# A four-layer convolution and attention trunk: three instead of four convolution tiles on TensorE, more taps on GpSimd, other PSUM banks for the output accumulators

## The chip, the cores and the metric

The kernel runs on one core of one Trainium2 chip. The metric is the device time of one execution in microseconds; lower is better. The core's engines run their own instruction queues in order and wait for one another through semaphores: PE (TensorE, matrix products), DVE (VectorE), ACT (ScalarE), POOL (GpSimd), and SP, which here only issues DMAs.

## The reference, cut to what matters

The input is 512 positions of 1024 channels. Four residual layers follow one another, of kinds A, B, C, A. Each computes x + Mixer(RMSNorm(x)); the inner width is 2048, so 16 tiles of 128 channels. The change concerns kind A, in layers 0 and 3:

```python
def conformer_conv_mixer(h, w_in, conv_w, conv_b, ln_g, ln_b, w_out):
    proj = h @ w_in
    val, glu_gate, z = jnp.split(proj, 3, axis=-1)
    u = val * jax.nn.sigmoid(glu_gate)
    u = causal_depthwise_conv(u, conv_w) + conv_b      # 31 taps, each channel by itself
    u = jax.nn.silu(layer_norm(u, ln_g, ln_b))         # over the 2048 channels
    return (u * jax.nn.silu(z)) @ w_out
```

Kind B is forgetting attention with 16 heads, kind C a short convolution of three taps. Both also end with a product by their `w_out`. All arithmetic is float32 in accuracy: each matrix product is made of three passes (high part by high part, high by low, low by high).

## The kernel before, in words

**Layout.** Everything stands transposed: 128 channels on the partitions, 512 positions along a row. Weights arrive in chunks of 128x1024 (`w_raw`). ACT casts a chunk to its high part (`w_hi`), and POOL or DVE subtracts to get the low part (`w_lo`, line 413). In an A layer, up to the layer norm, only POOL does that. A chunk feeds 24 products of 128x128 by 128x512 on PE, 8 in each of the three passes. An A layer uses 48 chunks for `val`, `gate` and `z` of the 16 tiles, and 16 chunks for the output product. `z` of a tile is multiplied nine tiles after its `val` and `gate` (`LAG`), so a stock of `z` products is left when the convolution ends.

**The convolution of a tile i.** ACT writes tap 0 into a PSUM bank (`cv`). DVE adds one tap after another there (`scalar_tensor_tensor`, line 341). The first `POOL_TAPS[i]` taps are taken from it: for each of them ACT writes u times the tap's weight (`prod`) and POOL adds it to `pacc` (line 330). At the end DVE adds `cv`, the bias and `pacc` to give `d`. Tile 0 has no POOL taps. Tiles in `PE_TILES` go another way (`conv_pe`): ACT reorders u, DMAs write it to DRAM and read it back as four phases, PE applies 36 matrices of 128x128 loaded by nine DMAs (`pw`, in a ring of 8 slots), and DMAs and ACT undo the reordering.

**The layer norm.** POOL sums the tiles and their squares into `s1` and `s2` (`count_in`); the last three tiles (`DIRECT`) are not added there. PE sums over the channels, with two products (`meanp`, `e2p`) for `s1`, `s2` and two more for each of the last three tiles. Tiles 0 to 3 and those on PE first get a shift `m0` added on POOL. From the sums ACT and DVE make `lnrp`, one over the standard deviation. Then for each tile DVE subtracts the mean and multiplies by `lnrp`, ACT applies SiLU, POOL multiplies by `sz` (SiLU of `z`; DVE does it for the first two tiles), and ACT and DVE split the result into `g_hi` and `g_lo`.

**The output product** (`out_projection`). Its first half runs over pairs of tiles and keeps four accumulators `o0` to `o3` open in four PSUM banks; each pair is 24 products. The second half makes `o4` to `o7` one after another.

**PSUM.** There are eight banks in five groups: `mm` has 3, `acc` 2, `tr`, `sum` and `o` one each. Within a group, banks are handed out in turn, and who gets one waits until its former user has been read. `val`, `gate` and `z` use `mm`. The convolution's tiles use `acc`, `o`, `acc`, `tr` in turn. `sum` holds `e2p`, `o` holds `meanp`, and the last user of `acc` ahead of the output product is `lnrp`.

**The order of the work.** All steps are recorded and then put in order by a planner (`Plan`), which has costs for each step and engine, priorities (`boost`) and numbers of slots; the order of each engine's queue is fixed when the program is built. Any change of taps or tiles thus moves many instructions.

Of the kernel before, what the change touches and what calls it, by code (L numbers as in the profile page):

```python
# [19 lines left out]
ND = D // P  # L20
# [5 lines left out]
NEG = -1e30  # L26
LAYERS = ("A", "B", "C", "A")
LAG = 9
POOL_TAPS = (0, 5, 5, 5, 5, 5, 5, 5, 5, 5, 5, 5, 5, 5, 5, 5)
PE_TILES = {0: (6, 10, 13, 15), 3: (6, 10, 13, 15)}  # L30
NP = 4
NL = (KC - 1 + NP - 1) // NP + 1

# [217 lines left out]
def trunk(ctx: ExitStack, tc: tile.TileContext, x, w, vec, pw, out):  # L251
# [14 lines left out]
    def name_(s):  # L266
        count[0] += 1
        return f"{s}_{count[0]}"

    def slot(name, dt=F32, ring=(None, 1)):  # L270
        n = name_(name)
        return plan.buf(lambda: big.tile([P, T], dt, tag="big", name=n, bufs=N_SLOTS), *ring,
                        slot=True)

    def psum(tag, name):
        n, k = name_(name), PSUM_BUFS[tag]
        return plan.buf(lambda: ps.tile([P, T], F32, tag=tag, name=n, bufs=k), "ps_" + tag, k)
# [15 lines left out]
    def pe_time(n):  # L293
        return max(0.108, 0.0105 + n * 0.4225e-3)
# [80 lines left out]
    def mms(jobs, dst, cost, reads, boost=0):  # L375

        def fn(e):
            for o, a, b, start, stop in jobs():
                nc.tensor.matmul(o, a, b, start=start, stop=stop)  # L379
        plan.op({"pe": cost}, fn, reads, dst, boost)  # L380
# [141 lines left out]
                hh[d], hl[d] = split(f, f"hn{self.layer}_{d}", ("dve",), boost=-2000)  # L522
            return hh, hl

    def out_projection(layer, gh, gl, make_g, spare_bank):

        last_layer = layer == len(LAYERS) - 1
        nxt = None if last_layer else Stream(layer + 1)
        half, pairs = ND // 2, NE // 2

        def evac(d, acc):
            tt(("dve",), xs[d], acc, xs[d], A.add)
            if last_layer:
                plan.op({"dma": 0.9}, lambda e, d=d: nc.sync.dma_start(out[d], xs[d]()), [xs[d]])
            else:
                nxt.add(d)

        accs = [psum("mm" if d < 3 else spare_bank, f"o{d}") for d in range(half)]
        for j in range(pairs):
            hi, lo = chunk()  # L540
            for kk in range(2):
                make_g(2 * j + kk)
            for g, (a, b) in enumerate(((hi, gh), (hi, gl), (lo, gh))):
                for kk in range(2):
                    k = 2 * j + kk
                    mms(lambda a=a, b=b, g=g, kk=kk, k=k: [
                            (accs[d](), a()[:, kk * 512 + d * P : kk * 512 + (d + 1) * P], b[k](),
                             k == 0 and g == 0, k == NE - 1 and g == 2) for d in range(half)],
                        accs, pe_time(T) * half, [a, b[k]])
        for d in range(half):  # L550
            evac(d, accs[d])
        for d, tag in zip(range(half, ND), ("o", "acc", "acc", "mm")):
            acc = psum(tag, f"o{d}")
            for hf in range(2):
                hi, lo = chunk()
                for g, (a, b) in enumerate(((hi, gh), (hi, gl), (lo, gh))):
                    mms(lambda a=a, b=b, g=g, hf=hf, acc=acc: [
                            (acc(), a()[:, k * P : (k + 1) * P], b[8 * hf + k](),
                             hf == 0 and k == 0 and g == 0, hf == 1 and k == 7 and g == 2)
                            for k in range(8)],  # L560
                        [acc], pe_time(T) * 8, [a, *(b[8 * hf + k] for k in range(8))])
            evac(d, acc)
        return nxt


    def conformer(layer, st):
        lo_engines["now"] = ("pool",)
        on_pe = PE_TILES[layer]
        FIRST, EARLY = 2, 7
        raw_tiles, SPREAD, SHIFTED, DIRECT = 2, 12, 4, 3  # L570

        def cw(i, s):
            return v(f"conv_w{layer}", i * KC + KC - 1 - s)
# [22 lines left out]
        def conv(i):  # L596

            n_pool = POOL_TAPS[i]
            pacc = pool_part(i, n_pool) if n_pool else None
# [10 lines left out]
        def conv_pe(i):  # L610


            n, m, C = on_pe.index(i), T // NP, P // NP
            first = -2000 if i == NE - 1 else 0
            u, acc = us[i], psum(tags[i % 4], f"cv{layer}_{i}")
            d2[i] = slot(f"d{i}")
            ua, r, oa, ob = (slot(nm) for nm in ("ua", "phases", "oa", "ob"))
            ud, od = (plan.buf(lambda nm=nm: scratch.tile([P, T], F32, name=nm))
                      for nm in (f"ud{layer}_{i}", f"od{layer}_{i}"))

            def swap(src, dram, dst):

                plan.op({"dma": 2.5}, lambda e: nc.sync.dma_start(dram(), src()), [src], [dram], first)
                for k in range(NP):
                    plan.op({"dma": 0.5 if k < NP - 1 else 1.5}, lambda e, k=k: nc.sync.dma_start(
                        dst()[k * C : (k + 1) * C, :].rearrange("c (a m) -> c a m", a=NP),
                        dram()[:, k * m : (k + 1) * m].rearrange("(a c) m -> c a m", a=NP)),
                        [dram], [dst], first)

            plan.op({"act": 0.65}, lambda e: nc.scalar.copy(  # L630
                ua()[:, :].rearrange("p (h m) -> p h m", h=NP),
                u()[:, :].rearrange("p (m h) -> p h m", h=NP)), [u], [ua], first)
            swap(ua, ud, r)
            jobs = [(g, lag) for g in range(NP) for lag in range(NL)]
            for k in range(0, len(jobs), 4):
                mats = slot("pw", ring=("pw", 8))
                plan.op({"dma": 0.8}, lambda e, mats=mats, k=k: nc.sync.dma_start(
                    mats(), pw[n if layer == 0 else len(PE_TILES[0]) + n, k // 4]), w=[mats])
                mms(lambda mats=mats, k=k: [
                        (acc()[:, g * m + lag : (g + 1) * m], mats()[:, q * P : (q + 1) * P],  # L640
                         r()[:, g * m : (g + 1) * m - lag], lag == 0, lag == NL - 1)
                        for q, (g, lag) in enumerate(jobs[k : k + 4])],
                    [acc], 0.87, [mats, r], boost=first or SPREAD * (k // 4))
            act(oa, acc, None, boost=first)
            swap(oa, od, ob)
            vb, at = v(f"conv_b{layer}", i)
            plan.op({"act": 0.7}, lambda e: nc.scalar.activation(
                d2[i]()[:, :].rearrange("p (m h) -> p h m", h=NP),
                ob()[:, :].rearrange("p (h m) -> p h m", h=NP), AF.Identity,
                bias=vb()[:, at]), [ob, vb], [d2[i]], first)  # L650
# [26 lines left out]
        for n, (name, i) in enumerate(order):  # L677
# [6 lines left out]
            acc = psum("mm", f"{name}{layer}_{i}")  # L684
# [4 lines left out]
            if raw:  # L689
                if name == "gate" and i == 0:  # L690
                    f = slot("raw")
                    tt(("dve",), f, vals[i], st.rstd, A.mult, boost=-2500)
                    vals[i] = f
                f = slot("raw")
                tt(("dve",), f, acc, st.rstd, A.mult, boost=-2500)
                acc = f
# [29 lines left out]
        gh, gl = {}, {}  # L726
# [9 lines left out]
            tt(("dve",) if first else ("pool",), f, f, sz[k], A.mult, boost=boost)  # L736
            gh[k], gl[k] = split(f, f"g{layer}_{k}", ("dve",), boost=boost)

        return out_projection(layer, gh, gl, make_g, "tr")


    def attention(layer, st):
# [7 lines left out]
        gs, gh, gl = {}, {}, {}  # L750
# [108 lines left out]
        def make_g(k):  # L859
            gh[k], gl[k] = split(gs[k], f"g{layer}_{k}", ("dve", "pool"))  # L860

        return out_projection(layer, gh, gl, make_g, "sum")


    def short_conv(layer, st):
        lo_engines["now"] = ("pool", "dve")
        h = (st.hh, st.hl)
        gh, gl = {}, {}
        for i in range(NE):
            up = psum("mm", f"u{i}")  # L870
            project(up, h, fine=i == 0)
            if i == 0:
                st.norm()
                rstd2 = slot("rstd2")
                tt(("dve",), rstd2, st.rstd, st.rstd, A.mult)
            u, cu, y, z = slot("u"), slot("cu"), slot("y"), slot("z")
            tt(("dve",), u, up, rstd2, A.mult)
            cp = psum("mm", f"c{i}")
            project(cp, h)
            tt(("dve",), cu, cp, u, A.mult)  # L880
            acc = psum("acc", f"sc{i}")
            ts(acc, cu, v("c_conv", i * 3 + 2), A.mult)
            for s in (1, 2):
                stt(acc, cu, v("c_conv", i * 3 + 2 - s), acc, A.mult, A.add, s=slice(0, T - s),
                    d=slice(s, T))
            tt(("dve",), y, acc, st.rstd, A.mult)
            bp = psum("mm", f"b{i}")
            project(bp, h)
            tt(("dve",), y, bp, y, A.mult)
            zp = psum("mm", f"z{i}")  # L890
            project(zp, h)
            tt(("dve",), z, zp, st.rstd, A.mult)
            act(z, z, AF.Silu)
            tt(("pool",), y, y, z, A.mult)
            gh[i], gl[i] = split(y, f"g{layer}_{i}", ("dve",))
        return out_projection(layer, gh, gl, lambda k: None, "sum")

    st = Stream(0)
    for d in range(ND):
# [103 lines left out]
```

## Time and profile before

| | |
|---|---|
| time, median of 3 runs | 1842.82 us (1841.53 to 1843.14) |
| the profiled execution: its time, and its span from first to last instruction | 1842.16 us, 1840.3 us |
| busy share of the span | PE 97%, DVE 67%, POOL 57%, ACT 47% |
| layer 0 (A), by the places of its first and last products | 0 to about 423 us |
| layers 1 and 2 (B, C) | about 423 to 1428 us |
| layer 3 (A) | about 1428 us to the end |

In a table of stretches, each engine has its busy time and, in brackets, the instructions that began there; PEclk is the granted TensorE clock as a share of full speed. In a timeline a row is start, duration, engine, line, operation, output<-inputs, shapes and count; brackets at its end hold the idle time ahead of it and what ended it. In a list of waits a row is the waiting engine and line, the one waited for, the total in us, how often, and the longest. In groups of instructions a row ends with busy us, mean ns of one, and idle time before them. Products of 512 columns in float32r take one record each, those in plain float32 (the sums, and the convolution's 128 columns) two.

### The profile page before, as it was taken

The page shows a single profiled execution, that of the slowest core. Times are in us where ns is not written, and L with a number is a line of the kernel's source. Part 1 is how long each engine was busy: PE and PEld are TensorE (multiplying, and loading weights), DVE is VectorE, ACT ScalarE, POOL GpSimd, SP SyncE. Part 2 cuts the span into 40 slices and gives each one's busy share as a digit, 9 for nine tenths or more (in the row PEclk, how much of TensorE's full clock was granted, in tenths as well). Part 3 has the DMA queues.
Part 4 walks back from the last instruction along what each step waited for, and adds up shares of the span by engine and source line. Part 5 has one row for each costly group of instructions (what it writes and reads, how often), then busy time and mean ns, then how long its engine had stood idle before and what let it go on. Part 6 is the DMA issues. An engine that isn't in the chain of part 4 may idle for free.

```text
span 1840.3 us, 21959 instructions
## 1 busy us (share of the span) xinstructions
PE 1790.1 (97%) x8252; PEld 1476.9 (80%) x8252; DVE 1233.3 (67%) x1692; ACT 856.7 (47%) x1213; POOL 1050.4 (57%) x601
## 2 busy tenths in 40 slices
PE   8999999899999999999999999999999999999899
PEld 6888787787788878878788888888888878887687
DVE  7999997436988888899723333334303899999820
ACT  6645546335656666666533222222223655563720
POOL 5997766654444434464454454545445598874842
PEclk9999999999999999999999999999999999999999
DMA  6244442223222222222222222232333224443221
GB/s 230 92 155 138 137 133 71 87 95 112 90 75 86 81 81 91 75 69 69 69 92 95 100 93 102 92 103 92 103 107 127 88 99 147 143 143 111 79 92 69
DMA packets 68537, 189.23 MB, mean 103 GB/s; under 512 B 7744, under 2 KB 15936, under 8 KB 68432
## 3 DMA queue, kind: packets, MB, share of 16 engines
q1 hardware_dynamic: 68432, 187.83, 30.2%
q8 instruction: 65, 1.06, 0.2%
q14 instruction: 40, 0.33, 0.1%
HBM read 181.48 MB, written 6.32 MB: 102 GB/s over the span
## 4 chain that ended last, share of the span: by engine, by line
PE 57%; DVE 24%; ACT 2%; issue 2%; DMA 0%; SPq 0%; DVEq 0%; ACTq 0%
PE o L379 19%; DVE cv L341 11%; PE z L379 10%; PE u L379 5%; PE c L379 5%; PE b L379 5%; PE q L379 3%; PE v L379 3%; PE k L379 2%; DVE p L823 2%; DVE d L330 2%; DVE g_lo L366 1%; DVE nmax L825 1%; DVE p L341 1%; DVE nt L341 1%
## 5 line engine op out<-in xcount | busy, mean ns | idle before, releaser
L413 POOL TENSOR_TENSOR w_lo<-w_raw,w_hi 128x1024 fp32r<-128x1024 f32 x286 | 691.3, 2418 | 620.1 <-PE o L379 112.2
L315 ACT CAST w_hi<-w_raw 128x1024 fp32r<-128x1024 f32 x289 | 303.2, 1049 | 577.2 <-PE o L379 150.3
L341 DVE SCALAR_TENSOR_TENSOR cv<-u,vt,cv 128x501 f32<-128x501 f32 (+5 forms) x610 | 449.3, 737 | 19.8
L330 DVE TENSOR_TENSOR x<-o,x 128x512 f32<-128x512 f32 x32 | 21.2, 687 | 241.4 <-PE o L379 241.4
L379 PE MATMUL o<-g_hi,w_hi 128*128 128x512 f32 x512 | 130.8, 397 | 12.7 <-ACT sz L317 12.4
L379 PE MATMUL o<-g_lo,w_hi 128*128 128x512 f32 x512 | 129.7, 396 | 0.0
L379 PE MATMUL o<-g_hi,w_lo 128*128 128x512 f32 x512 | 127.1, 390 | 0.0
L379 PEld LDWEIGHTS o<-g_hi,w_hi 128*128 128x128 f32 x512 | 97.3, 191 | 34.5 <-ACT sz L317 13.2
L379 PEld LDWEIGHTS o<-g_lo,w_hi 128*128 128x128 f32 x512 | 98.2, 192 | 20.8
L330 POOL TENSOR_TENSOR pacc<-prod,pacc 128x510 f32<-128x510 f32 (+1 forms) x88 | 104.3, 1186 | 16.0 <-ACT prod L317 11.9
L379 PEld LDWEIGHTS o<-g_hi,w_lo 128*128 128x128 f32 x512 | 95.9, 188 | 19.9
L246 ACT ACT_TABLE_LOAD x70 | 89.8, 1283 | 1.9 <-PEq L991 0.7
L317 ACT ACTIVATE prod<-u,vt 128x510 f32<-128x510 f32 (+4 forms) x104 | 67.5, 710 | 38.8 <-DVE u L330 38.7
L379 PEld LDWEIGHTS cv<-phases,pw 128*128 128x128 f32 x576 | 70.4, 199 | 13.8 <-DVE d L341 7.0
L379 PE MATMUL cv<-phases,pw 128*128 128x128 f32 (+8 forms) x576 | 71.5, 283 | 9.4 <-DVE d L341 5.8
L330 DVE TENSOR_TENSOR z<-z,rstd 128x512 f32<-128x512 f32 x32 | 22.0, 688 | 77.0 <-PE z L379 77.0
L366 POOL TENSOR_TENSOR sq_lo<-sq,sq_hi 128x512 fp32r<-128x512 f32 x29 | 39.7, 1368 | 49.6 <-ACT sq_hi L315 46.4
L379 PE MATMUL z<-hh,w_lo 128*128 128x512 f32 x256 | 64.9, 395 | 0.0
L379 PE MATMUL z<-hn_hi,w_hi 128*128 128x512 f32 x256 | 64.8, 395 | 0.0
L379 PE MATMUL z<-hn_lo,w_hi 128*128 128x512 f32 x256 | 64.2, 393 | 0.0
L379 PE MATMUL z<-hl,w_hi 128*128 128x512 f32 x256 | 63.5, 390 | 0.0
L379 PE MATMUL z<-hh,w_hi 128*128 128x512 f32 x256 | 63.4, 390 | 0.0
(243 smaller groups left out, 3812.2 us busy)
## 6 DMA issues: line engine op xcount, KB each, us to landing
w_raw<-w SPq DMA_DIRECT2D x289, 512.0 KB, 3.2
pw<-pw SPq DMA_DIRECT2D x72, 256.0 KB, 4.3
nc<-cd SPq DMA_DIRECT2D x16, 256.0 KB, 3.8
x<-x SPq DMA_DIRECT2D x8, 256.0 KB, 5.1
ud<-ua SPq DMA_DIRECT2D x8, 256.0 KB, 2.2
phases<-ud SPq DMA_DIRECT2D x32, 64.0 KB, 2.2
od<-oa SPq DMA_DIRECT2D x8, 256.0 KB, 3.8
ob<-od SPq DMA_DIRECT2D x32, 64.0 KB, 1.9
```

The lines of the kernel that those rows point to most:

```text
L246: switch(table)
L315: nc.scalar.copy(of(dst, d), of(src, s))
L317: nc.scalar.activation(of(dst, d), of(src, s), func, **kw)
L330: eng[e].tensor_tensor(of(dst, d), of(a, s), of(b, sb), op)
L341: nc.vector.scalar_tensor_tensor(of(dst, d), of(a, s), c, bb.bitcast(F32) if b_f32r else bb, op0, op1)
L366: eng[e].tensor_tensor(of(lo, d), of(src, s), of(hi, d).bitcast(F32), A.subtract)
L379: nc.tensor.matmul(o, a, b, start=start, stop=stop)
L413: eng[e].tensor_tensor(lo(), raw(), hi().bitcast(F32), A.subtract)
L823: plan.op({"dve": 0.2}, lambda e, i=i: nc.vector.tensor_tensor(p[i]()[:, blk(i)], p[i]()[:, blk(i)], mask(), A.add), [p[i], mask], [p[i]])
L825: plan.op({"dve": dve_time(n)}, lambda e, i=i, s=s: nc.vector.tensor_reduce(nmax[i](), p[i]()[:, s], mybir.AxisListType.X, A.max, negate=T ...
```

## The change

In layers 0 and 3 alike: tiles 7, 12 and 15 go to PE instead of 6, 10, 13 and 15. The other tiles but 0 give POOL seven taps instead of five, and tile 14 nine. The ring of `pw` has 5 slots instead of 8. Only the last two tiles are summed directly on PE (`DIRECT` 2). The output accumulators of the A layers stand in the banks `sum`, `tr`, `acc`, `mm` and then `o`, `mm`, `mm`, `acc`, instead of `mm`, `mm`, `mm`, `tr` and `o`, `acc`, `acc`, `mm`. Layers B and C get their banks by the new argument too, but the same ones as before, and the order of their instructions is the same as before on all engines.

```diff
-POOL_TAPS = (0, 5, 5, 5, 5, 5, 5, 5, 5, 5, 5, 5, 5, 5, 5, 5)
-PE_TILES = {0: (6, 10, 13, 15), 3: (6, 10, 13, 15)}
+POOL_TAPS = (0, 7, 7, 7, 7, 7, 7, 7, 7, 7, 7, 7, 7, 7, 9, 7)
+PE_TILES = {0: (7, 12, 15), 3: (7, 12, 15)}
...
-    def out_projection(layer, gh, gl, make_g, spare_bank):
+    def out_projection(layer, gh, gl, make_g, banks):
...
-        accs = [psum("mm" if d < 3 else spare_bank, f"o{d}") for d in range(half)]
+        accs = [psum(banks[d], f"o{d}") for d in range(half)]
...
-        for d, tag in zip(range(half, ND), ("o", "acc", "acc", "mm")):
-            acc = psum(tag, f"o{d}")
+        for d in range(half, ND):
+            acc = psum(banks[d], f"o{d}")
...
-        raw_tiles, SPREAD, SHIFTED, DIRECT = 2, 12, 4, 3
+        raw_tiles, SPREAD, SHIFTED, DIRECT = 2, 12, 4, 2
...
-                mats = slot("pw", ring=("pw", 8))
+                mats = slot("pw", ring=("pw", 5))
...
-        return out_projection(layer, gh, gl, make_g, "tr")
+        return out_projection(layer, gh, gl, make_g, ("sum", "tr", "acc", "mm", "o", "mm", "mm", "acc"))
```

How this moves instructions, at three places of layer 0 (layer 3 is alike). Names end in numbers of the program's own; `z0_12` is `z` of layer 0, tile 12.

**PE, from the last sums to the output product, before.** Between the last sum and the first product of `o0` stand 136 products of `z`, from the middle of tile 10 to tile 15.

```order
L379 MATMUL meanp_339_2462<-d14_295_2566,ones_e_11_75 128x512
L379 MATMUL e2p_340_2466<-sq_296_2572,ones_e_11_75 128x512
L379 MATMUL meanp_339_2462<-d15_304_2523,ones_e_11_75 128x512
L379 MATMUL e2p_340_2466<-sq_318_2568,ones_e_11_75 128x512
L379 MATMUL z0_10_327_2574<-hn0_0_lo_55_280,w_hi42_2345 128x512
...
L379 MATMUL z0_15_337_2827<-hn0_7_hi_75_410,w_lo47_2678 128x512
L379 MATMUL o0_345_2889<-g0_0_hi_349_2685,w_hi48_2713 128x512
L379 MATMUL o1_346_2890<-g0_0_hi_349_2685,w_hi48_2713 128x512
L379 MATMUL o2_347_2891<-g0_0_hi_349_2685,w_hi48_2713 128x512
```

The same place in the changed kernel:

```order
L379 MATMUL meanp_358_2560<-d14_314_2669,ones_e_11_75 128x512
L379 MATMUL e2p_359_2568<-sq_315_2679,ones_e_11_75 128x512
L379 MATMUL meanp_358_2560<-d15_323_2565,ones_e_11_75 128x512
L379 MATMUL e2p_359_2568<-sq_337_2598,ones_e_11_75 128x512
L379 MATMUL z0_12_350_2656<-hn0_0_hi_54_276,w_lo44_2522 128x512
...
L379 MATMUL z0_15_356_2802<-hn0_7_hi_75_404,w_lo47_2667 128x512
L379 MATMUL o0_364_2851<-g0_0_hi_368_2792,w_hi48_2686 128x512
L379 MATMUL o1_365_2852<-g0_0_hi_368_2792,w_hi48_2686 128x512
L379 MATMUL o2_366_2853<-g0_0_hi_368_2792,w_hi48_2686 128x512
```

Now 80 products of `z` stand there, from the last pass of tile 12 on: 56 have moved ahead of the sums.

**POOL, at the end of the convolution, before.** The last POOL taps, those of tile 14 (`pacc_288`), stand 13 instructions ahead of the shift of `d15`.

```order
L330 TENSOR_TENSOR pacc_288_1517<-prod_292_2142,pacc_288_1517 128x508
L330 TENSOR_TENSOR pacc_288_1517<-prod_293_2151,pacc_288_1517 128x507
L413 TENSOR_TENSOR w_lo39_2211<-w_raw39_2025,w_hi39_2196 128x1024
L413 TENSOR_TENSOR w_lo40_2260<-w_raw40_2068,w_hi40_2234 128x1024
L330 TENSOR_TENSOR s1_44_707<-s1_44_707,d11_243_2249 128x512
L330 TENSOR_TENSOR s2_45_709<-s2_45_709,sq_244_2263 128x512
...
L413 TENSOR_TENSOR w_lo44_2537<-w_raw44_2328,w_hi44_2520 128x1024
L330 TENSOR_TENSOR d15_304_2523<-d15_304_2523,m0_46_661 128x512
```

The same end in the changed kernel (`pacc_303` is tile 14's):

```order
L413 TENSOR_TENSOR w_lo45_2570<-w_raw45_2379,w_hi45_2553 128x1024
L330 TENSOR_TENSOR d15_323_2565<-d15_323_2565,m0_46_665 128x512
L330 TENSOR_TENSOR pacc_303_2483<-prod_308_2205,pacc_303_2483 128x507
L330 TENSOR_TENSOR pacc_303_2483<-prod_309_2208,pacc_303_2483 128x506
L330 TENSOR_TENSOR pacc_303_2483<-prod_310_2220,pacc_303_2483 128x505
L413 TENSOR_TENSOR w_lo46_2628<-w_raw46_2431,w_hi46_2609 128x1024
L330 TENSOR_TENSOR pacc_303_2483<-prod_311_2225,pacc_303_2483 128x504
L330 TENSOR_TENSOR pacc_303_2483<-prod_312_2236,pacc_303_2483 128x503
```

The last taps of tile 14 now come behind the shift of `d15`, the last of them six instructions behind it.

**SP, the matrices of tile 15, before.** Eight of the nine loads (`pw_309` to `pw_316`) stand ahead of the phases of that tile (`phases_306`); one, `pw_317`, stands far behind them.

```order
L637 DMA pw_314_2173<-pw 128x512
L399 DMA w_raw42_2228<-w 128x1024
L637 DMA pw_315_2246<-pw 128x512
L399 DMA w_raw43_2277<-w 128x1024
L637 DMA pw_316_2310<-pw 128x512
L399 DMA w_raw44_2328<-w 128x1024
L623 DMA ud0_15_2334<-ua_305_2331 128x512
L625 DMA phases_306_2360<-ud0_15_2334 32x4x128 x4
```

In the changed kernel the loads are `pw_328` to `pw_336`, and behind the phases stand:

```order
L625 DMA phases_325_2375<-ud0_15_2354 32x4x128 x3
L399 DMA w_raw46_2431<-w 128x1024
L637 DMA pw_333_2442<-pw 128x512
L637 DMA pw_334_2449<-pw 128x512
L637 DMA pw_335_2457<-pw 128x512
L637 DMA pw_336_2465<-pw 128x512
L623 DMA od0_15_2505<-oa_326_2502 128x512
```

Four loads of tile 15 now wait until its own first products free their slots.

More of the change, by code (lines that the diff above doesn't have):

```diff
@@ L860, in make_g @@
             gh[k], gl[k] = split(gs[k], f"g{layer}_{k}", ("dve", "pool"))
-        return out_projection(layer, gh, gl, make_g, "sum")
+        return out_projection(layer, gh, gl, make_g, ("mm", "mm", "mm", "sum", "o", "acc", "acc", "mm"))
     def short_conv(layer, st):
@@ L895, in short_conv @@
             gh[i], gl[i] = split(y, f"g{layer}_{i}", ("dve",))
-        return out_projection(layer, gh, gl, lambda k: None, "sum")
+        return out_projection(layer, gh, gl, lambda k: None,
+                              ("mm", "mm", "mm", "sum", "o", "acc", "acc", "mm"))
     st = Stream(0)
```

## The prediction

> **What bounds the kernel now.** I began with the page's busy times, then went to the stretches of the A layers, the list of waits, the chain, and the timelines around the end of the convolution.
>
> ```profile
> PE 1790.1 (97%) x8252; PEld 1476.9 (80%) x8252; DVE 1233.3 (67%) x1692; ACT 856.7 (47%) x1213; POOL 1050.4 (57%) x601
> 60.00:100.00 40.00, 39.28 (x172) 31.88 (x171) 38.38 (x54) 22.46 (x33) 37.55 (x28) 1.00 0.29 96
> 100.00:140.00 40.00, 40.00 (x215) 34.48 (x214) 38.20 (x54) 18.68 (x26) 35.58 (x29) 1.00 0.48 162
> 320.00:340.00 20.00, 13.82 (x50) 10.90 (x49) 19.93 (x21) 12.45 (x20) 17.27 (x11) 0.83 0.23 80
> PE o L379 <- ACT sz L317: 12.4, 2, 6.2
> PE cv L379 <- DVE d L341: 5.8, 3, 2.9
> PE cv L379 <- DMA phases<-ud: 3.6, 2, 2.2
> ```
>
> The columns of a stretch are its length, then PE, weight loads, DVE, ACT, POOL, clock, DMA. The reader is to see three things. PE fills the span. In the convolution of an A layer (second and third row) DVE is 96% busy as well and POOL 91%, so three engines are near full at once; ACT has room. And PE's largest single wait is not in the convolution but at the start of the output product: 6.2 us in each A layer, put down to the SiLU of `z`. Layers B and C keep their instructions and their order, so I give them no change.
>
> The end of the convolution in layer 0, on PE, DVE and ACT:
>
> ```profile
> 290.24 0.75 DVE L341 SCALAR_TENSOR_TENSOR d<-cv,vt,pacc 128x512 f32<-128x512 f32 x1 [0.19 <-DVE cv L341]
> ...
> 292.51 1.02 PE L379 MATMUL meanp<-d,ones_e 128*128 128x512 f32 x2
> ...
> 295.08 1.02 PE L379 MATMUL e2p<-sq,ones_e 128*128 128x512 f32 x2
> 295.54 2.40 PE L379 MATMUL z<-hn_lo,w_hi 128*128 128x512 f32 x8
> 297.78 1.98 PE L379 MATMUL z<-hn_hi,w_lo 128*128 128x512 f32 x8
> 299.59 1.98 PE L379 MATMUL z<-hn_hi,w_hi 128*128 128x512 f32 x8
> ...
> 326.79 0.61 PE L379 MATMUL o<-g_hi,w_hi 128*128 128x512 f32 x2
> 333.58 2.93 PE L379 MATMUL o<-g_hi,w_hi 128*128 128x512 f32 x6 [6.18 <-ACT sz L317]
> ...
> 333.58 89.48 PE o L379 x382
> 332.23 0.81 ACT L317 ACTIVATE d<-d,vt 128x512 f32<-128x512 f32 x1 [0.64 <-DVE d L330]
> 332.95 0.58 ACT L317 ACTIVATE sz<-z 128x512 f32<-128x512 f32 x1
> ```
>
> DVE finishes tile 14 at 291.0, the last sum begins at 295.08, and at 295.54 (I call this moment T0) PE turns to its stock of `z`. It works that off, starts two products of the output, and stands still until ACT has emptied the bank of the last `z`. ACT had that SiLU queued behind one that waited for DVE. Layer 3 repeats it.
>
> ```profile
> 1708.45 2.40 PE L379 MATMUL z<-hn_lo,w_hi 128*128 128x512 f32 x8
> ...
> 1746.50 2.93 PE L379 MATMUL o<-g_hi,w_hi 128*128 128x512 f32 x6 [6.18 <-ACT sz L317]
> ```
>
> From T0 to the resumption it is 38.04 us in layer 0 and 38.05 in layer 3.
>
> **The change, part by part, for one A layer.**
>
> *Stock of `z`.* Behind T0 there are 80 products instead of 136. Eight take 1.81 us (297.78 to 299.59), so 0.227 each: 56 fewer start the output product 12.7 us earlier after T0. The room for them ahead of T0 comes from the tile that leaves PE and from one pair of sums.
>
> *Banks.* `o0` to `o2` no longer take the banks of tiles 13 to 15's `z`; only `o3` takes one, that of tile 13, whose SiLU now stands ahead of those that give the first `g`. The other three banks belonged to `e2p`, tile 15's `cv` and tile 14's `cv`, all read by then. I take the whole 6.2 us as gone. What is late next is the supply of `g`, below.
>
> *Clock.* After that stop PE ran slowly: 382 products at 0.227 would be 86.7 us, the chain shows 89.48. So 2.8 us go too.
>
> ```profile
> 334.00:336.00 2.00, 2.00 (x6) 0.50 0.05 12
> ...
> 338.00:340.00 2.00, 2.00 (x8) 0.71 0.43 174
> 1679.00:1682.00 3.00, 2.51 (x16) 0.76 0.49 182
> 1679.49 9.01 PE L379 MATMUL cv<-phases,pw 128*128 128x128 f32 x64 [2.25 <-DMA phases<-ud]
> ```
>
> In these rows of PE alone the clock is the third figure from the end; 0.50 and 0.71 behind the stop are what the 2.8 us come from. The Trainium skill (TensorE: Matmul & The Clock Gate, section Why this matters for your kernels) says to avoid pauses of PE of more than about 3 us, since one costs the full clock. The 6.2 us stop agrees with it; but here a pause of 2.25 us also brought 0.76. By the page short new pauses cost only themselves and the sum below stands; by the row (64 records in 9.01 us, against 7.30 in the next fence) one more such pause a layer costs 1.7 us each, and the sum would be 1813.
>
> *T0 itself.* These 21.7 us (12.7 + 6.2 + 2.8) hold if T0 stays. Three engines can push it out.
>
> ```profile
> 266.97 7.30 PE L379 MATMUL cv<-phases,pw 128*128 128x128 f32 x64
> 72.33:290.24 217.91, 165.22 (x116) 0.99 0.40 132
> L330 POOL TENSOR_TENSOR pacc<-prod,pacc 128x510 f32<-128x510 f32 (+1 forms) x88 | 104.3, 1186 | 16.0 <-ACT prod L317 11.9
> L413 POOL TENSOR_TENSOR w_lo<-w_raw,w_hi 128x1024 fp32r<-128x1024 f32 x286 | 691.3, 2418 | 620.1 <-PE o L379 112.2
> L330 POOL TENSOR_TENSOR s<-s,d 128x512 f32<-128x512 f32 x24 | 30.9, 1289 | 26.5 <-DVE d L341 26.2
> L341 DVE SCALAR_TENSOR_TENSOR cv<-u,vt,cv 128x501 f32<-128x501 f32 (+5 forms) x610 | 449.3, 737 | 19.8
> L317 ACT ACTIVATE prod<-u,vt 128x510 f32<-128x510 f32 (+4 forms) x104 | 67.5, 710 | 38.8 <-DVE u L330 38.7
> DMA to landing us min/median/max: 3.4/4.3/6.3
> ```
>
> DVE: its taps are 30 + 11·25 = 305 before and 30 + 11·23 + 21 = 304 after, with one more closing `d`; at 0.74 each that is nothing, and DVE ran back to back (19.8 us idle ahead of 610 taps). So DVE alone leaves T0 where it is.
>
> PE: ahead of T0 it gains 56 `z` (12.7), loses 36 matrices (72 records; 64 take 7.30, so 8.2) and one pair of sums (two of 0.86, the step from 292.51 over three sums to 295.08; 1.7). That is 2.8 more. Four of tile 15's nine matrix loads now wait for its own first products; they land in 3.4 to 6.3 us (last row, all loads of `pw`) while five of nine groups of products last 4.6, so 0 to 3 us of stop, most often 1. Against this, PE's waits of today for a bank and the phases (5.8 and 3.6 us over both layers) have one tile fewer to occur at. PE may be 0 to 6 us late.
>
> POOL: between the shift of `d0` (72.33) and the closing `d` of tile 14 (290.24) it was busy 165.2 of 217.9 us. By the order, up to tile 14's last tap it now does 29 more adds (34.4), two more `w_lo` (4.8), two more sums (2.6) and one shift less (1.3): 205.7, which leaves 12.2 us for waits. In 60 to 140, where it was fullest, it was idle 6.9 of 80 us, 8.6%; in the first half of that 6.1%. On 217.9 us that is 13 to 19, so POOL closes tile 14 about 1 to 7 us late.
>
> These run side by side, so the latest counts, not their sum: 4 us, in the middle of both; ends 0 and 8.
>
> ACT writes 31 more `prod` at 0.71, 22 us, and saves one tile's reorderings; with 22.5 of 40 us busy it has the room, and DVE, which reads none of them, covers it; without that cover POOL would feel it, which is in its waits. DMAs fall by 19 (nine `pw`, ten for the swaps). SP's queue holds little behind the four late loads: tile 15's own return and two `w_raw`, needed after the sums.
>
> *Supply of `g`.* The output product starts about 18.5 us after T0 and takes a pair every 5.4.
>
> ```profile
> 305.66 3.32 DVE L330 TENSOR_TENSOR d<-d,sz 128x512 f32<-128x512 f32 x2
> 309.06 1.30 DVE L366 TENSOR_TENSOR g_lo<-d,g_hi 128x512 fp32r<-128x512 f32 x2
> 310.28 2.47 DVE L330 TENSOR_TENSOR d<-d,lnrp 128x512 f32<-128x512 f32 x4
> 312.67 1.98 DVE L366 TENSOR_TENSOR g_lo<-d,g_hi 128x512 fp32r<-128x512 f32 x1
> ...
> 329.81 1.79 DVE L366 TENSOR_TENSOR g_lo<-d,g_hi 128x512 fp32r<-128x512 f32 x1
> ...
> 334.04 2.25 DVE L413 TENSOR_TENSOR w_lo<-w_raw,w_hi 128x1024 fp32r<-128x1024 f32 x1
> 336.20 4.78 DVE L366 TENSOR_TENSOR g_lo<-d,g_hi 128x512 fp32r<-128x512 f32 x6
> ```
>
> Before, the first two `g_lo` were there 14.8 us after T0, the eighth at 36.1 and the fourteenth at 45.4; PE took them up only at 38. Now the fourth pair begins at 18.5 + 16.3 = 34.8 and wants its `g_lo` 1.8 later, 36.6. One `w_lo` (2.25) now stands ahead of the fifth to eighth `g_lo` on DVE, and two products of 0.62 stand behind them that stood ahead: 36.1 + 2.25 - 1.2 = 37.2, 0.6 late. With some unevenness in the pairs ahead I take 1.5 us, ends 0 and 6 (a `w_lo` of 2.25 and four slow subtractions, 1.9 instead of 0.8, are 6.6).
>
> **Sum.** 21.7 - 4 - 1.5 = 16.2 us a layer, 32.4 in all. The profiled execution took 1842.16 us, 0.66 below the median of the runs. 1842.2 - 32.4 gives 1809.8; I say 1810.
>
> **The rivals.**
>
> *POOL closes the convolution.* If it keeps half of the 52.7 us that it was idle in that stretch, 26, it is 14 us late: 21.7 - 14 - 1.5 = 6.2 a layer, 1829.8. For it: it must be busy 94% of the stretch, and it waits in order for DVE's `d` (26.2 us before the sums alone). Against: an engine with a backlog finds its inputs ready, as in 60 to 100.
>
> *The same, so far that the kernel is slower.* POOL also makes every `w_lo`, so its lateness reaches PE's products, and through `u` DVE. If all 52.7 us of idle stay, T0 is 40.5 late and a layer loses 20.3: 1882.8. It decides from 20.2 us of lateness, 32 us of idle time, on.
>
> *The supply of `g` sets the output product.* With 6 instead of 1.5 us: 11.7 a layer, 1818.8. For it, the rows of 1.8 and 1.98 us, against 0.8 in the group of six that began when POOL was nearly through. The Trainium skill (GPSIMD Engine Reference, section Key points) has GpSimd share its memory interfaces with VectorE, with contention where a VectorE instruction has two inputs in SBUF; the rows agree, and the taps, with one input in PSUM, are spared. Against it: after the fourth pair POOL's products end and DVE gets ahead.
>
> *The bank change does nothing*, since `o3` still wants a `mm` bank: the 9.0 us of stop and slow clock stay, 7.2 a layer, 1827.8. Against: tile 13's `z` is multiplied two tiles earlier and its SiLU precedes work that the first `g` needs anyway.
>
> **Chances.** The forecast 0.56, with a range of its own from 1799 (T0 and the supply cost nothing: 2 times 21.7 is 43.4) to 1818. Supply 0.12, POOL closing 0.16, banks 0.05, slower 0.11. The range 1799 to 1832 takes in all but the slower case. A measurement of this kernel can tell about 0.2% from no change. Slower by more has 0.08; within, 0.04 (0.03 of the last case and the edge of POOL closing); faster 0.88.
>
> **What would show it.** Right: no wait of `o` for `sz`; 80 `z` between sums and `o`, which starts near T0 + 18.5; the clock at 1.00 there; T0 of layer 0 between 295 and 304; POOL over 90% busy from 72 us to T0. DVE's row for tile 14's `d` tells the cases apart: with idle time ahead of it, released by POOL, POOL closes the convolution. Wrong: PE waiting for POOL's `w_lo` in the convolution, or `o` waiting for `g_lo` by more than 6 us a layer.

## The result, and the profile after

| | before | after |
|---|---|---|
| time, median of 4 runs | 1842.17 us (1841.07 to 1843.14) | 1800.07 us (1798.12 to 1802.08) |
| ratio, with its 95% interval | | 0.977 (0.976 to 0.979) |
| profiled execution: time, span | 1842.16, 1840.3 us | 1798.12, 1796.0 us |

The changed kernel is 42.1 us faster. The two A layers account for that, so the table of stretches is the first view to read. For each kernel, row 1 is layer 0 up to T0 (the first `z` behind the last sums), row 2 from T0 to the next layer's first product; rows 3 and 4 are the same for layer 3, from its first product to the start of the last group of products. Before:

```profile
20.00:295.54 275.54, 269.65 (x1310) 224.85 (x1308) 257.31 (x356) 145.79 (x191) 202.43 (x137) 0.99 0.39 132
295.54:422.90 127.36, 121.18 (x523) 99.62 (x521) 60.24 (x67) 58.77 (x79) 82.60 (x43) 0.97 0.26 89
1428.14:1708.45 280.31, 273.85 (x1326) 227.71 (x1324) 258.93 (x357) 148.25 (x194) 203.86 (x136) 0.99 0.37 122
1708.45:1836.07 127.62, 121.44 (x522) 99.45 (x520) 47.88 (x58) 46.15 (x61) 68.14 (x36) 0.97 0.23 79
```

After:

```profile
20.00:296.45 276.45, 272.38 (x1290) 224.96 (x1289) 256.89 (x356) 166.05 (x225) 243.95 (x172) 1.00 0.38 124
296.45:402.05 105.60, 105.60 (x466) 87.28 (x465) 65.79 (x68) 54.78 (x74) 77.44 (x40) 1.00 0.29 95
1405.62:1686.56 280.94, 275.79 (x1305) 227.82 (x1304) 258.45 (x357) 168.37 (x228) 245.83 (x171) 1.00 0.35 117
1686.56:1792.33 105.77, 105.77 (x466) 87.07 (x464) 53.34 (x59) 42.19 (x56) 62.99 (x33) 1.00 0.25 82
```

The reader is to see that T0 hardly moved (0.91 us later in layer 0, 0.63 in layer 3), and that the part behind it is 21.76 and 21.85 us shorter, with PE busy all of it at a clock of 1.00. The two layers gain 20.85 and 21.22, together 42.07. The two spans differ by some 2 us more than that, mostly in layers B and C, whose instructions are the same: single executions differ by that much (the four of the changed kernel by 4 us), and the medians don't show it.

The busy times and the group of POOL's taps, 148 instead of 88, of the page:

```profile
PE 1762.0 (98%) x8100; PEld 1451.0 (81%) x8100; DVE 1242.8 (69%) x1694; ACT 889.3 (50%) x1271; POOL 1123.4 (63%) x665
...
L330 POOL TENSOR_TENSOR pacc<-prod,pacc 128x510 f32<-128x510 f32 (+5 forms) x148 | 175.1, 1184 | 11.1 <-ACT prod L317 4.5
```

DVE and PE at the end of layer 0's convolution, and the piece of the chain that begins there:

```profile
290.20 0.75 DVE L341 SCALAR_TENSOR_TENSOR d<-cv,vt,pacc 128x512 f32<-128x512 f32 x1
...
324.31 6.88 DVE L366 TENSOR_TENSOR g_lo<-d,g_hi 128x512 fp32r<-128x512 f32 x4
...
293.42 1.02 PE L379 MATMUL meanp<-d,ones_e 128*128 128x512 f32 x2
...
296.45 2.40 PE L379 MATMUL z<-hn_hi,w_lo 128*128 128x512 f32 x8
...
315.01 1.98 PE L379 MATMUL o<-g_hi,w_hi 128*128 128x512 f32 x8
```

```profile
315.17 87.04 PE o L379 x384
```

`o` starts 18.56 us after T0 and is not interrupted: neither a bank nor a `g` is waited for (no number in brackets), and the chain has 384 products in one piece, at 0.227 us each. Tile 14's `d` on DVE starts at 290.20 as before the change (290.24), with no idle time ahead of it, so POOL, with seven taps a tile (nine for this one), was not late. PE began the sums 3.2 us after that, at 293.42, without a wait: its own work set T0. POOL came close to being late, as the same stretch of POOL's work shows in both kernels (before, then after; POOL is the last engine):

```profile
71.21:290.24 219.03, 213.86 (x1073) 180.49 (x1072) 209.04 (x290) 112.09 (x142) 166.34 (x116) 0.99 0.40 132
```

```profile
71.21:290.20 218.99, 215.67 (x1049) 179.85 (x1048) 208.84 (x290) 128.44 (x171) 204.46 (x149) 1.00 0.38 125
```

POOL went from 166 to 204 us of 219. Its idle time fell from 52.7 to 14.5 us.

### The profile page after: what moved, and what is told of

Read it like the earlier page. It is cut to its first block, busy times and chain, and to the rows that moved or that the text cites. A ratio compares the mean times of both kernels' runs of the same rounds, so it can differ in the third digit from the quotient of the medians.

```text
span 1796.0 us, 21693 instructions
## 1 busy us (share of the span) xinstructions
PE 1762.0 (98%) x8100; PEld 1451.0 (81%) x8100; DVE 1242.8 (69%) x1694; ACT 889.3 (50%) x1271; POOL 1123.4 (63%) x665
## 4 chain that ended last, share of the span: by engine, by line
PE 68%; DVE 26%; POOL 2%; issue 2%; ACT 2%; DMA 1%; SPq 0%; DVEq 0%; POOLq 0%; ACTq 0%
PE o L379 19%; PE z L379 14%; DVE cv L341 14%; PE u L379 5%; PE c L379 5%; PE b L379 5%; PE q L379 3%; PE v L379 3%; PE gate L379 3%; PE val L379 3%; PE k L379 2%; DVE p L823 2%; PE cv L379 1%; DVE p L341 1%; DVE nmax L825 1%
## 5 line engine op out<-in xcount | busy, mean ns | idle before, releaser
L341 DVE SCALAR_TENSOR_TENSOR cv<-u,vt,cv 128x495 f32<-128x495 f32 (+24 forms) x608 | 447.2, 736 | 19.7
L330 POOL TENSOR_TENSOR pacc<-prod,pacc 128x510 f32<-128x510 f32 (+5 forms) x148 | 175.1, 1184 | 11.1 <-ACT prod L317 4.5
L317 ACT ACTIVATE prod<-u,vt 128x510 f32<-128x510 f32 (+8 forms) x166 | 106.8, 709 | 49.7 <-DVE u L330 49.7
L379 PE MATMUL z<-hn_hi,w_lo 128*128 128x512 f32 x256 | 64.3, 393 | 0.0
L317 ACT ACTIVATE p<-p,nmax 128x512 f32<-128x512 f32 (+1 forms) x64 | 36.0, 563 | 55.1 <-DVE nmax L825 55.0
```

What stands on the lines that cost most here:

```text
L317: nc.scalar.activation(of(dst, d), of(src, s), func, **kw)
L330: eng[e].tensor_tensor(of(dst, d), of(a, s), of(b, sb), op)
L341: nc.vector.scalar_tensor_tensor(of(dst, d), of(a, s), c, bb.bitcast(F32) if b_f32r else bb, op0, op1)
```

## The experiments

The theory: in an A layer PE's own work, plus its few stops, sets the time, as long as enough `z` is left behind the last sums to cover the layer norm, and as long as DVE and POOL close the convolution by then. The rivals: POOL is what limits the changed kernel; DVE is; the banks make all of the gain or none of it. In each job the kernel before was run as well; its medians were 1840.5 to 1841.4 us. The changed kernel's 1800.07 comes from the first table, where the kernel before had 1842.2; so by the times alone a difference of 2 us or less from it says nothing.

### The banks alone

```diff
 (the kernel before)
-        return out_projection(layer, gh, gl, make_g, "tr")
+        return out_projection(layer, gh, gl, make_g, ("sum", "tr", "acc", "mm", "o", "mm", "mm", "acc"))
```

> The kernel before with only the new PSUM banks of the output accumulators in layers 0 and 3; taps, tiles, ring of pw and direct sums as before, and the same order of instructions. Theory (PE is the bound of the A layers, so what it no longer stands or runs slowly for is gained): the 6.2 us stop at the start of the output product and the 2.8 us of slow clock behind it go in each A layer, 18 us in all, 1824; no wait of the output product for g, since its g were ahead. Rival (the stop only hid the supply of g): the wait goes over to g_lo and most of the 18 us stay, 1835 to 1842. Rival (all of the gain comes from the banks): 1800.

Measured: 1823.16 us (1822.75 to 1824.42), ratio 0.990 (0.989 to 0.992). PE at the output product of layer 0, and the next layer's first product:

```profile
295.10 1.02 PE L379 MATMUL e2p<-sq,ones_e 128*128 128x512 f32 x2
...
326.81 1.98 PE L379 MATMUL o<-g_hi,w_hi 128*128 128x512 f32 x8
...
413.85 1.76 PE L379 MATMUL f<-hh,w_hi 128*128 128x512 f32 x7
```

`o` begins at the same time as before (326.8) and runs on; the next layer starts at 413.85 instead of 422.90. So 9.05 us a layer are the stop of 6.2 and the slow clock behind it: with no stop there is no slow clock.

### The changed kernel with the old banks

```diff
-        return out_projection(layer, gh, gl, make_g, ("sum", "tr", "acc", "mm", "o", "mm", "mm", "acc"))
+        return out_projection(layer, gh, gl, make_g, ("mm", "mm", "mm", "tr", "o", "acc", "acc", "mm"))
```

> The changed kernel with the old banks (mm, mm, mm, tr and o, acc, acc, mm) for the output accumulators. Theory: the stop comes back, since the third accumulator takes the bank of tile 15's z; but ACT has that SiLU earlier in its queue now, behind four SiLUs of d, a cast and g_hi of tile 2, so 2 to 6 us a layer with the slow clock instead of 9: 1804 to 1812. Rival (the two parts add up without touching each other): 9.0 a layer, 1818. Rival (banks count for nothing): 1800.

Measured: 1801.96 us (1801.43 to 1803.84), ratio 0.979 (0.978 to 0.980). PE, ACT and the chain in layer 0:

```profile
314.90 0.61 PE L379 MATMUL o<-g_hi,w_hi 128*128 128x512 f32 x2
316.44 1.66 PE L379 MATMUL o<-g_hi,w_hi 128*128 128x512 f32 x6 [0.93 <-ACT sz L317]
...
315.81 0.59 ACT L317 ACTIVATE sz<-z 128x512 f32<-128x512 f32 x1
```

```profile
316.44 86.88 PE o L379 x382
```

This is 2 us below the range expected, and nearer to the rival that banks count for nothing: the stop was priced too high. The wait for the last SiLU is still there, but it is 0.93 instead of 6.18 us, because ACT reaches that SiLU 0.9 us after the product starts, with no idle time ahead of it; before, ACT had waited for DVE there. No slow clock follows (86.88 for 382). So, by layer 0 of the traces, the banks are worth 9 us on the old order of work and about 1 on the new one (the medians, 1.9 us apart, can't tell it from nothing): the new order alone takes away most of the same stop. The two parts don't add up: alone they give 17 and 39 us, together 42.

### Four tiles on PE instead of three

```diff
-PE_TILES = {0: (7, 12, 15), 3: (7, 12, 15)}
+PE_TILES = {0: (6, 10, 13, 15), 3: (6, 10, 13, 15)}
```

> The changed kernel with the four tiles 6, 10, 13 and 15 on PE again; taps 7 (and 9 for tile 14), banks, ring and two direct sums as changed. DVE loses 23 taps and a closing d a layer (17.7 us), POOL seven adds (8.3), PE gains 36 matrices (8.2). Theory (PE's own work sets when the output product starts): 8.2 us a layer more, 1816, with 120 to 136 products of z between the sums and the output. Rival (DVE or POOL closing the convolution sets it): not slower, 1782 to 1800.

Measured: 1817.47 us (1815.31 to 1818.58), ratio 0.987 (0.986 to 0.989): 17.4 us above the changed kernel, or 8.7 a layer. Thirty-six matrices are 8.2. DVE closes its last tile early, which helps nothing:

```profile
271.77 0.75 DVE L341 SCALAR_TENSOR_TENSOR d<-cv,vt,pacc 128x512 f32<-128x512 f32 x1
...
324.21 1.98 PE L379 MATMUL o<-g_hi,w_hi 128*128 128x512 f32 x8
```

`o` starts 9.2 us later than in the changed kernel, with 136 products of `z` behind the sums. Relieving DVE and POOL buys nothing while PE has that work to do.

### One POOL tap more, and one fewer

```diff
-POOL_TAPS = (0, 7, 7, 7, 7, 7, 7, 7, 7, 7, 7, 7, 7, 7, 9, 7)
+POOL_TAPS = (0, 8, 8, 8, 8, 8, 8, 8, 8, 8, 8, 8, 8, 8, 10, 8)
```

> The changed kernel with one more tap on POOL for each of the 12 DVE tiles (8, and 10 for tile 14): POOL gets 12 adds a layer more (14.2 us), DVE 12 taps less (8.8). In the changed kernel POOL was idle 14.5 us of the 219 us of its convolution, and its last add ended 0.2 us before tile 14 closed. Theory (POOL is just in time): its waits cannot all go, so tile 14 closes 5 to 14 us late in each layer, 1810 to 1828, with DVE idle ahead of tile 14's d, released by POOL. Rival (PE alone is the bound, POOL has room): 1798 to 1802.

Measured: 1829.85 us (1828.63 to 1831.3), ratio 0.994 (0.993 to 0.996), some 2 us above the range expected. DVE's last closings and PE in layer 0, and the stretch of POOL's work:

```profile
286.09 0.75 DVE L341 SCALAR_TENSOR_TENSOR d<-cv,vt,pacc 128x512 f32<-128x512 f32 x1 [5.61 <-POOL pacc L330]
303.07 0.75 DVE L341 SCALAR_TENSOR_TENSOR d<-cv,vt,pacc 128x512 f32<-128x512 f32 x1 [16.23 <-POOL pacc L330]
...
201.05 3.54 PE L379 MATMUL val<-hn_hi,w_hi 128*128 128x512 f32 x8 [4.68 <-DVE u L330]
219.85 5.46 PE L379 MATMUL cv<-phases,pw 128*128 128x128 f32 x24 [4.09 <-DMA phases<-ud]
...
306.55 1.02 PE L379 MATMUL meanp<-d,ones_e 128*128 128x512 f32 x2
```

```profile
71.21:290.20 218.99, 205.61 (x961) 171.09 (x960) 200.94 (x280) 122.62 (x171) 205.17 (x148) 0.98 0.34 113
```

One tap a tile further, POOL closes the convolution: twelve adds of 1.18 us are 14.2 us, and tile 14 closes 12.9 us later than in the changed kernel (303.07 against 290.20), DVE waiting. In the same stretch POOL got only 0.7 us more done than with seven taps (205.17 against 204.46): its 14 us of idle time do not shrink. But PE stopped as well, twice for over 4 us, each with a slow clock behind it; the first stop is for a `u` that stood behind some twelve taps in DVE's queue, where DVE was not idle. So two causes lie side by side. POOL's alone would keep the sums from beginning ahead of 304 us, 11 later than in the changed kernel. But PE did not wait for it there: it was at work until it began them at 306.55, 13.1 later. In this run PE's own stops and the slow clock behind them took the time (layer 0 has 10.6 us more of idle time on PE than the changed kernel, and 6.1 more of busy time), and these the expectation did not have. That POOL alone would have cost those 11 us is argued and not shown.

```diff
-POOL_TAPS = (0, 7, 7, 7, 7, 7, 7, 7, 7, 7, 7, 7, 7, 7, 9, 7)
+POOL_TAPS = (0, 6, 6, 6, 6, 6, 6, 6, 6, 6, 6, 6, 6, 6, 8, 6)
```

> The changed kernel with one POOL tap fewer in each of the twelve tiles on DVE: six instead of seven, tile 14 eight. POOL has 12 adds of 1.18 us less (14.2 us a layer), DVE 12 taps of 0.74 us more (8.9 us), PE the same work. By the order 56 products of z (48 in layer 3) stand behind the last sums instead of 80, so they are worth 12.7 and 10.9 us instead of 18.2. Theory (PE's own work sets the layer, as long as enough z is left to cover the layer norm; in the changed kernel the first g_lo comes about 14.6 us after T0): DVE closes tile 14 near 300 instead of 291 us, T0 comes about 7 us later, the stock of z ends before the first g is there, and PE waits 2 to 6 us a layer: 1804 to 1812 us, POOL with 25 us or more of idle time. Rival 1 (POOL closes the convolution in the changed kernel and is what limits it): faster, 1796 or less. Rival 2 (PE's work alone, whatever the order): 1800.

Measured: 1807.37 us (1804.44 to 1808.65), ratio 0.982 (0.980 to 0.983), within the theory's range. DVE and PE in layer 0, and the stretch:

```profile
299.12 0.75 DVE L341 SCALAR_TENSOR_TENSOR d<-cv,vt,pacc 128x512 f32<-128x512 f32 x1 [0.19 <-DVE cv L341]
...
262.94 7.38 PE L379 MATMUL cv<-phases,pw 128*128 128x128 f32 x64 [1.79 <-issue]
272.07 1.15 PE L379 MATMUL cv<-phases,pw 128*128 128x123 f32 x8 [1.74 <-DMA pw<-pw]
...
322.88 2.43 PE L379 MATMUL o<-g_hi,w_hi 128*128 128x512 f32 x8 [0.89 <-ACT g_hi L315]
...
326.45 1.19 PE L379 MATMUL o<-g_lo,w_hi 128*128 128x512 f32 x4 [0.22 <-DVE g_lo L366]
```

```profile
71.21:290.20 218.99, 213.52 (x1045) 179.27 (x1044) 209.46 (x290) 123.35 (x160) 191.32 (x137) 1.00 0.38 125
```

POOL has 27.7 us of idle time, and the kernel is slower, so POOL alone did not limit the changed kernel. DVE closes tile 14 8.9 us later, and 24 products of `z` are spent while it does, after which `o` waits for `g`. That wait is 1.3 us in all; the rest of the 4.1 us that layer 0 is longer are mostly waits of PE ahead of and in tile 15's matrices (the rows of 1.79 and 1.74; the same matrices had one wait, of 0.78, in the changed kernel). The total was as expected, but partly by luck, since the wait for `g` was smaller than the 2 to 6 us given to it. Six, seven and eight taps give 1807, 1800 and 1830 us. On either side one of the two engines closes tile 14 late, and on either side much of the loss is PE's stops at other places.

### Sums on PE: one tile, or three, instead of two

```diff
-        raw_tiles, SPREAD, SHIFTED, DIRECT = 2, 12, 4, 2
+        raw_tiles, SPREAD, SHIFTED, DIRECT = 2, 12, 4, 3
```

> The changed kernel with three tiles summed directly on PE as before the change (DIRECT 3): PE one pair of sums more (1.7 us a layer), POOL two sums less (2.6 us). 104 products of z (96 in layer 3) stand behind the last sums, more than the layer norm needs. Theory (PE's own work sets the layer): 1803.5, no wait of o. Rival (POOL, just in time in the changed kernel, sets it): 1795 to 1800.

Measured: 1803.73 us (1803.06 to 1807.44), ratio 0.980 (0.979 to 0.982). The theory's time to 0.3 us; POOL's 3 us less work in the stretch (201.46 instead of 204.46) bought nothing.

With `DIRECT` 1:

> The changed kernel with only the last tile summed directly on PE (DIRECT 1): PE has one pair of sums less (1.7 us a layer), POOL two sums more (2.6 us), one of them behind the closing d of tile 14. By the order 48 products of z stand behind the last sums instead of 80. Theory (PE's work sets the layer only while the z left covers the layer norm, about 14.6 us from T0 to the first g_lo): 48 products cover 10.9 us, so o waits about 4 us for g, less 1.7: 1802 to 1808 us. Rival 1 (PE's work alone): 1796.6. Rival 2 (POOL just in time, every us of it counts): 1805, with T0 waiting for POOL's s and not o for g.

Measured: 1800.85 us (1795.68 to 1803.47), ratio 0.978 (0.976 to 0.980): just below the expected range, and not to be told from the changed kernel. DVE and PE in layer 0:

```profile
291.90 0.75 DVE L341 SCALAR_TENSOR_TENSOR d<-cv,vt,pacc 128x512 f32<-128x512 f32 x1 [2.46 <-POOL pacc L330]
...
312.69 1.09 PE L379 MATMUL o<-g_hi,w_hi 128*128 128x512 f32 x4
314.17 1.19 PE L379 MATMUL o<-g_hi,w_hi 128*128 128x512 f32 x4 [0.38 <-ACT g_hi L315]
...
323.48 1.20 PE L379 MATMUL o<-g_lo,w_hi 128*128 128x512 f32 x4 [1.38 <-DVE g_lo L366]
402.50 1.76 PE L379 MATMUL f<-hh,w_hi 128*128 128x512 f32 x7
```

The mechanism is the expected one, its size is not. POOL was 2.46 us late for tile 14, which cost nothing, since PE still had `z` to do ahead of the sums. `o` then waited for `g`, but 1.8 us and not 4, about what the spared pair of sums is worth (1.7): the next layer starts 0.45 us later than in the changed kernel (402.50 against 402.05). PE's work alone would have given 1796.6.

### Eight slots for the matrices instead of five

```diff
-                mats = slot("pw", ring=("pw", 5))
+                mats = slot("pw", ring=("pw", 8))
```

> The changed kernel with eight slots for the matrices pw instead of five, so that no load of tile 15 has to wait for three groups of its own products. PE's work is the same. The waits for late matrices were 0 in layer 0 and 0.4 and 1.1 us in layer 3 of the changed kernel. Theory (PE's work and its few stops set the time): 1798.5 to 1800. Rival, the step of the prediction that gave such loads 1 us a layer: 1798. A time that differs by more than 2 us comes from the other order of the instructions, to be seen in the waits.

Measured: 1820.21 us (1818.55 to 1820.81), ratio 0.989 (0.987 to 0.991). This missed both expectations by 20 us. The planner put the work in another order on all engines; PE, and then ACT, in layer 3:

```profile
1660.20 3.78 PE L379 MATMUL z<-hn_hi,w_hi 128*128 128x512 f32 x8 [9.96 <-ACT sz L317]
1663.78 3.19 PE L379 MATMUL z<-hn_lo,w_hi 128*128 128x512 f32 x8
...
1649.78 1.05 ACT L315 CAST w_hi<-w_raw 128x1024 fp32r<-128x1024 f32 x1 [5.33 <-DMA w_raw<-w]
...
1657.02 0.63 ACT L317 ACTIVATE sq<-d 128x512 f32<-128x512 f32 x1 [4.42 <-POOL d L330]
...
1659.55 0.60 ACT L317 ACTIVATE sz<-z 128x512 f32<-128x512 f32 x1
```

PE needs a bank of `mm`; the SiLU that empties it stands in ACT's queue behind a square that waits for POOL's shift, after ACT had come late to this stretch through a wait for a weight chunk (5.33 us). With the slow clock behind it (sixteen products in 6.6 us, where 3.6 is usual) the stop is about 13 of the 20 us. It is the same kind of stop as the one that the change removed, at another place and longer. What the late loads of `pw` cost was thus not measured by itself: the rows of the changed kernel hold 1.4 us for both layers together.

### Seven taps for tile 14 as well

```diff
-POOL_TAPS = (0, 7, 7, 7, 7, 7, 7, 7, 7, 7, 7, 7, 7, 7, 9, 7)
+POOL_TAPS = (0, 7, 7, 7, 7, 7, 7, 7, 7, 7, 7, 7, 7, 7, 7, 7)
```

> The changed kernel with seven POOL taps for tile 14 as for the others, instead of nine: POOL two adds of 1.18 us less a layer (2.4 us), DVE two taps of 0.74 more (1.5 us), PE the same work; 88 products of z behind the last sums instead of 80 (20.0 instead of 18.2 us), enough to cover the layer norm. Theory (PE's own work sets the layer, DVE and POOL just keep up): 1800, between 1799 and 1803, POOL with some 2 us more of idle time. Rival 1 (POOL just in time at tile 14 is what limits the changed kernel): 2 x 2.4 less, 1795. Rival 2 (DVE's taps limit it): 2 x 1.5 more, 1803. A stop of more than 2 us by a SiLU of z that stands behind waiting work in ACT's queue, as with eight slots of pw, would add itself and is to be seen in the waits.

Measured: 1803.22 us (1798.98 to 1806.02), ratio 0.980 (0.978 to 0.981). This is just above the theory's range, at the time of the rival that DVE's taps count, and little more than 2 us from the changed kernel. The waits ahead of the last sums in both layers favour that rival here:

```profile
292.59 1.12 PE L379 MATMUL meanp<-d,ones_e 128*128 128x512 f32 x2 [0.71 <-DVE gq L746]
...
1682.61 1.12 PE L379 MATMUL meanp<-d,ones_e 128*128 128x512 f32 x2 [1.16 <-DVE d L341]
```

In the changed kernel PE did not wait there: its sums began 3.2 us after tile 14's `d` (293.42 and 290.20). With two taps more on DVE and 8 products of `z` less ahead of the sums, it waits. That POOL sets the time (1795) is excluded: it had 2.2 us more of idle time in the stretch, and the kernel was not faster. None of the nine beat the changed kernel.

### All runs as PE's ledger

Layer 0, from 20 us to the next layer's first product, out of the same view of stretches for each kernel; idle is length less busy.

| | length | PE busy | PE idle |
|---|---|---|---|
| before | 402.9 | 390.8 | 12.1 |
| before, new banks | 393.9 | 388.1 | 5.7 |
| after | 382.1 | 378.0 | 4.1 |
| after, old banks | 383.2 | 378.3 | 4.9 |
| four tiles on PE | 391.3 | 387.1 | 4.2 |
| eight POOL taps | 398.8 | 384.1 | 14.7 |
| six POOL taps | 386.2 | 378.7 | 7.5 |
| `DIRECT` 3 | 385.2 | 380.2 | 5.0 |
| `DIRECT` 1 | 382.5 | 376.3 | 6.2 |
| eight slots | 386.3 | 380.1 | 6.2 |
| seven taps for tile 14 too | 383.1 | 377.8 | 5.3 |

PE's busy share is 96 to 99% in every row. The kernels differ by work given to PE (four tiles, `DIRECT`), by its stops, and by the slow clock behind the long ones, which counts as busy (before, eight taps, eight slots). DVE and POOL enter only as a cause of stops. A length is always busy plus idle time, so the table sorts the costs and does not prove the theory; what bears it out is that PE has little idle time in every kernel (4 to 15 us of some 390), and that its busy time goes with the work given to it.

## Why the prediction was right, and where its sizes were off

**Behind T0** the sum was right. It had 12.7 (stock), 6.2 (stop) and 2.8 us (clock), 21.7 a layer; 21.76 and 21.85 were measured. `o` started 18.56 us after T0, forecast 18.5. The stop and the clock were shown by the banks alone. The price of PE's tile behind the stock was shown by the kernel with four tiles. But as the old banks showed, the bank term belongs to the banks only on the old order of work; in the changed kernel most of the stop would have gone without them, which the step on banks did not see.

**T0 itself** is the first mis-sized term: forecast 4 us late, measured 0.91 and 0.63. The sides taken for PE and POOL were both too high. PE's busy time ahead of T0 grew by 2.73 us in layer 0, forecast 2.8. That this came out so near is partly luck: in the kernel before, the busy time also held 1.6 us of slow clock behind a stop of 2.89 us (56 records in 8.10 us, against 6.52; the rows are in the last section), which the forecast did not take off. PE's idle time there did not grow by the 1 us given to the late matrix loads: by the stretches it fell, from 5.89 (275.54 less 269.65) to 4.07 us, with one tile fewer to wait for banks and phases. POOL's lateness, forecast 1 to 7 us, was 0. It was 204.5 us busy, forecast 205.7, and idle 14.5, forecast 13 to 19. The method (the idle share of its fullest stretch, taken over the whole convolution) held here, and the true value lay at the low end. In the run with eight taps the idle time was about the same, 13.8 us; that it is a floor is not shown, since PE's stops fell into that stretch too.

**Supply of `g`**, forecast 1.5 us, cost nothing. The four `g_lo` that began at 324.31, those of tiles 4 to 7, were through at 331.2, where the fourth pair (tiles 6 and 7), at 315.0 + 16.3 + 1.8 by the prediction's pace, wanted them from 333.1 on. This leaves 1.9 us. The third pair was closer, which the prediction did not look at:

```profile
327.70 1.98 PE L379 MATMUL o<-g_lo,w_hi 128*128 128x512 f32 x8
```

Tile 5's subtraction, the second of the four, was through about 327.8 (half of 6.88 us behind 324.31), and PE wanted its result for the fifth of these eight products, at about 328.6. So some 0.8 us were left, and the supply was nearer to a wait than the fourth pair tells. The subtractions did take the slow 1.7 us each that the rival feared (6.88 for four). The runs with six taps and with `DIRECT` 1, whose stock was 56 and 48 products, show the wait that would have come: 1.3 and 1.8 us in layer 0.

Those two terms, 5.5 us a layer forecast and 0.6 to 0.9 measured, are nearly the whole difference between 1810 and 1800 (2 x 4.7 us).

**The rivals.** POOL closing the convolution: not here, but one tap a tile further DVE did wait for it (16.23 us), though PE, held up by its own stops, reached the sums later still (1830 us). The supply: not here, real but small with a smaller stock. The bank change doing nothing: wrong, as forecast, on the old order; nearly true in the changed kernel, for a reason other than the one given. The clock: a pause of 1.05 us, the longest between 20 us and T0 in layer 0, left it at 1.00 in the stretch (first row of after), so the term for new short pauses stayed at nothing, as the sum had it.

## What to carry to other kernels

When three engines are near full, price a shift of work on each of them, and take the idle share of the engine's fullest stretch as an estimate of what will be left of its idle time: here it fitted with seven taps and with eight. Count the work that covers a serial stage (here the `z` behind the sums) against that stage's length; more of it than that buys nothing, less becomes a wait. And where a planner orders everything, a stop seen in one build may come from the order of one queue: test a part of a change both alone and left out, for the two answers can differ widely (here 9 and 1 us a layer).

## What the runs showed of the hardware

**PE's clock and the length of a pause.** Eight products of `z`, `gate` or `val` after a pause, in layer 0 of the kernel with eight slots, and of that with eight taps (whose row of 4.68 us stands above):

```profile
186.51 2.11 PE L379 MATMUL gate<-hn_hi,w_hi 128*128 128x512 f32 x8 [0.75 <-ACT sg L317]
...
194.83 3.50 PE L379 MATMUL val<-hn_hi,w_hi 128*128 128x512 f32 x8 [2.58 <-DVE u L330]
```

```profile
172.92 2.11 PE L379 MATMUL z<-hn_hi,w_hi 128*128 128x512 f32 x8 [1.24 <-ACT sz L317]
```

Pauses up to 1.24 us left the next eight products at 2.11 us; pauses of 2.58 and 4.68 us both made them 3.5. Two rows of the kernel before, from layers 0 and 3, narrow this:

```profile
229.99 8.10 PE L379 MATMUL cv<-phases,pw 128*128 128x128 f32 x56 [2.89 <-DVE d L341]
...
1643.49 6.52 PE L379 MATMUL cv<-phases,pw 128*128 128x128 f32 x56 [1.79 <-DVE d L341]
```

A pause of 1.79 us left 56 records at 6.52 us (1.84 us, in the kernel with the new banks alone, did so too), one of 2.89 us made them 8.10. So in these runs the point from which a slow start is paid lies between 1.84 and, with the 2.25 us of the kernel before, about 2.3 us. The Trainium skill (TensorE: Matmul & The Clock Gate, section Why this matters for your kernels) puts it at about 3 us; here the measurement decides.

The price does not follow the length of the pause. It was 1.4 to 1.7 us behind 2.25, 2.58, 2.89 and 4.68 us. But it was about 2.7 behind 4.09 us (24 records in 5.46 us, where the pace of the row of 6.52 gives 2.8) and 2.8 behind the 6.18 us of the kernel before. What decides between the two sizes, no run here shows.
